# Layer 1 of a hybrid diffusion backbone: head outputs kept in SBUF, queries and key copies issued at other places, convolution outputs split later

## The chip, the cores and the metric

The kernel runs on one core of a Trainium2 chip. The time is that of the device, in microseconds (us), from the start of the program to its end. A core has five engines, each with its own in-order instruction stream: TensorE (PE, matrix products; its weight loads are listed apart as PEld), VectorE (DVE), ScalarE (ACT), GpSimd (POOL) and SyncE (SP, which here only issues transfers). An instruction whose operands are not ready holds up everything behind it on its engine. Transfers (DMAs) are issued from SP's and ACT's streams and run beside the engines. SBUF is the on-chip memory, PSUM the eight banks into which PE writes, DRAM the memory outside.

## The reference

Two layers over 1024 latent tokens of width 1024 and a prefix of 256 context tokens. Layer 0 holds two kinds of grouped-query attention and a projection. Layer 1, in which the edits lie, has a convolution branch C and a neighbourhood attention D over a grid of 16 rows and 64 columns:

```python
cv, cgl, cg, dq, dk, dv, dg = split_cols(h_lat @ w_in, ODD_WIDTHS)
oc = conformer_conv(cv, cgl, cg, dw_w, dw_b, ln_g, ln_b)
...
def d_row(args):      # one grid row of 64 queries; 8 heads
    kk = jnp.concatenate([c_dk, kr], axis=1)      # 256 context keys, 8 grid rows of keys
    vv = jnp.concatenate([c_dv, vr], axis=1)
    return gqa_attend(qr[:, :, :, None, :], kk, vv, bias).reshape(bsz, GRID_W, D_W)
...
y_lat = jnp.concatenate([oc, od * jax.nn.silu(dg)], axis=-1) @ w_out
x_lat = x_lat + g_l[:, None, :] * y_lat
```

`conformer_conv` is a depthwise convolution of 31 taps over 512 channels, a layer norm over the channels, and two SiLU gates. `gqa_attend` is softmax(q k / 8 + bias) v. All inputs and the output are float32; the output is an RMS norm of `x_lat`.

## The kernel before, in words

**Products in three parts.** Every float32 product is made of three matmuls on rounded numbers: `split` (line 294) writes the high part of a tile (a cast on ACT) and the low part (a subtraction on POOL, "g", or DVE, "v"), and `mm3` (line 315) issues high x high, high x low and low x high. So each tile that is to be multiplied costs an ACT cast and a POOL or DVE subtraction first, and both wait for the tile.

**Layer 1 in its order.** First the four blocks of the convolution's projection with the convolution itself (`conv_proj`, `conv_steps`, pool "cv"); then `d_proj(0)` and `d_proj(1)`, each of which projects q, k, v and gate of two of the eight heads and stores them in DRAM (QD, KD, VD, GD). Beside `d_proj(1)` runs the layer norm of the convolution (`ln_steps`, pool "ln"), whose result goes to DRAM too (Oc). Then the attention begins: 16 groups, each one head and one half of the grid's columns (`SEQ`). Three more pieces of work are woven between its steps by `weave`: `d_proj(2)`, `d_proj(3)`, and the output projection `out1_part`, first of the convolution's four blocks, then of the finished heads. `WV` holds how many steps of the attention go with each piece.

**One attention group.** `attn_prep` loads the group's queries (QH, QL), finds the row maxima on PE and DVE (`maxes`: product `mx`, then DVE's reductions with the bias tile `bm`), transposes them (`trn`) and writes them into QL, so that the softmax's shift is part of the score product. `attn_gen` then goes through seven tiles: two score matmuls `st` (QH with key tile KA, QL with key tile KB), the bias added on DVE (`pf`), the exponential on ACT, `split` into `ph` and `pl`, and some steps later three value matmuls `ov`. After the last tile `finish` divides, gates (`gt`) and stores. The preparation of group g+2 runs in the steps of group g. KB's upper part is a copy of KA on ACT (`load_k`, line 376), issued right behind the loads of KA, when the first group of the head before starts.

**Bounces through DRAM.** Each of the first six heads' outputs `y` is stored to O1d and comes back by `od_load`, which casts it on ACT. The convolution's outputs come back from Oc in `out1_alloc` and are split there, before the output projection is woven.

**What sets the order.** The program is handed to a scheduler which puts each engine's instructions into an order by priorities and by its own estimate of when each is ready; `later` and `issue_after` change a piece's priority or pin it behind a named instruction. So an edit at one place can move instructions at another, in layer 0 too. Memory pools lie on a stack: a tile whose bytes belonged to a pool before waits for the last use of those bytes. Of transfers on one stream, eight are under way at most (the ninth waits for the first's landing).

## Time and profile before

| | |
|---|---|
| time, median of 3 runs | 1595.98 us (1594.56 to 1597.62) |
| the profiled execution's own time | 1590.1 us |
| its span, first to last instruction | 1588.3 us |
| mean granted TensorE clock | 0.959 |
| busy: PE, PEld, DVE, ACT, POOL | 1477.4, 1178.0, 1087.8, 745.3, 791.0 us |
| first score matmul of layer 1's attention | at 1236.99 us of the span |
| bytes moved | 211.38 MB, mean 133 GB/s |

Times inside the program are microseconds from the start of the span. A row of the view by stretches gives, for each engine, the microseconds in which it was busy and the count of its instructions, then the granted clock (1.00 is full speed), and the share of time and rate of the transfers. A row of the view of waits names who waited, on what the wait ended, the sum, the number of times and the longest. A row of the chain has start, length and what ran; the chain follows back from the end to whatever released each step.

### The profile page before, as it was taken

The numbers are of one execution on the slowest core, as the hardware profiler recorded it, in microseconds if no ns is written. First come the engines' busy times: TensorE is split into PE (matmuls) and PEld (weight loads), VectorE is DVE, ScalarE is ACT, GpSimd is POOL, SyncE is SP. The second block draws the span as 40 slices with busy tenths as digits, with TensorE's granted clock in tenths as the row PEclk, the third lists the DMA queues.
The fourth block names the chain that finished last, engine by engine and source line by source line (L and its number), as shares of the span: only waits on it lengthen the run. The fifth ranks groups of instructions, "written<-read, shape, count | busy, mean of one in ns | idle before, by whom it ended". The sixth has DMA issues, their size and how long they took to land.

```text
span 1588.3 us, 21721 instructions
## 1 busy us (share of the span) xinstructions
PE 1477.4 (93%) x7084; PEld 1178.0 (74%) x7084; DVE 1087.8 (68%) x2283; ACT 745.3 (47%) x1418; POOL 791.0 (50%) x633
## 2 busy tenths in 40 slices
PE   6899999999999999999989879999998899899995
PEld 2785988886886778876866657888877778777775
DVE  2833576588599855566778857999566465778776
ACT  3722334443435555457555754433333454545563
POOL 3531352553445676557555755654431343344575
PEclk7899999998999999999999989999999899899997
DMA  9473324422312363212112032213546877988732
GB/s 366 157 238 121 110 84 152 137 76 90 110 50 82 99 210 101 64 57 65 30 38 80 7 101 60 80 54 101 190 160 198 234 222 215 273 243 239 224 101 106
DMA packets 159929, 211.38 MB, mean 133 GB/s; under 512 B 15356, under 2 KB 96456, under 8 KB 159816
## 3 DMA queue, kind: packets, MB, share of 16 engines
q1 hardware_dynamic: 153152, 198.42, 39.8%
q10 hardware_dynamic: 6664, 11.57, 2.2%
q8 instruction: 56, 0.92, 0.3%
q14 instruction: 57, 0.47, 0.1%
HBM read 153.84 MB, written 54.79 MB: 131 GB/s over the span
## 4 chain that ended last, share of the span: by engine, by line
PE 67%; DVE 16%; DMA 7%; issue 4%; ACT 2%; POOL 2%; SPq 0%; DVEq 0%; ACTq 0%; POOLq 0%
PE p L316 6%; PE p L317 6%; PE p L318 6%; PE ov L426 4%; PE ov L428 4%; PE ov L427 4%; PE st L463 4%; PE st L467 3%; PE po L316 3%; PE po L317 3%; PE po L318 3%; PE pq L316 3%; PE pq L317 3%; PE pq L318 3%; PE pg L318 2%
## 5 line engine op out<-in xcount | busy, mean ns | idle before, releaser
L299 POOL TENSOR_TENSOR pl<-pf,ph 128x512 fp32r<-128x512 f32 (+4 forms) x321 | 393.8, 1238 | 361.5 <-ACT ph L296 289.4
L299 POOL TENSOR_TENSOR wl<-wr,wh 128x512 fp32r<-128x512 f32 (+2 forms) x131 | 170.6, 1314 | 181.1 <-ACT wh L296 150.6
L475 ACT ACTIVATE pf<-st 128x512 f32<-128x512 f32 x284 | 165.6, 596 | 200.7 <-PE st L467 153.0
L296 ACT CAST ph<-pf 128x512 fp32r<-128x512 f32 (+4 forms) x364 | 209.6, 588 | 27.9 <-PE ov L427 17.7
L316 PE MATMUL p<-hh,wh 128*128 128x512 f32 x448 | 180.1, 402 | 8.6 <-ACT hh L296 2.8
L317 PE MATMUL p<-hl,wh 128*128 128x512 f32 x448 | 178.7, 400 | 0.9 <-POOL hl L299 0.9
L318 PE MATMUL p<-hh,wl 128*128 128x512 f32 x448 | 176.4, 400 | 0.0
L463 PE MATMUL st<-QH,KAt 128*128 128x512 f32 (+4 forms) x364 | 142.6, 393 | 10.0 <-ACT pf L475 8.1
L426 PE MATMUL ov<-ph,Vt 128*128 128x512 f32 (+4 forms) x364 | 141.3, 388 | 7.8 <-DVE y L625 6.2
L428 PE MATMUL ov<-pl,Vt 128*128 128x512 f32 (+4 forms) x364 | 141.6, 389 | 1.6 <-POOL pl L299 0.9
L427 PE MATMUL ov<-ph,Vt 128*64 128x512 f32 (+4 forms) x364 | 139.8, 384 | 0.0
L467 PE MATMUL st<-QL,KBt 68*128 68x512 f32 (+4 forms) x364 | 136.6, 388 | 0.0
L1041 DVE SCALAR_TENSOR_TENSOR cps<-U,taps,cps 128x512 f32<-128x512 f32 x184 | 126.4, 751 | 0.9
L296 ACT CAST wh<-wr 128x512 fp32r<-128x512 f32 (+2 forms) x134 | 81.1, 613 | 88.8 <-PE p L317 19.9
L316 PEld LDWEIGHTS p<-hh,wh 128*128 128x128 f32 x448 | 85.5, 191 | 31.3 <-ACT hh L296 3.0
L588 DVE TENSOR_REDUCE mp<-mx 128x1 f32<-128x512 f32 x128 | 85.9, 683 | 28.1 <-PE mx L587 27.5
L317 PEld LDWEIGHTS p<-hl,wh 128*128 128x128 f32 x448 | 85.1, 190 | 21.8 <-POOL hl L299 1.9
L318 PEld LDWEIGHTS p<-hh,wl 128*128 128x128 f32 x448 | 85.1, 190 | 19.9
L316 PE MATMUL pq<-wh,hh 128*128 128x384 f32 x256 | 88.4, 345 | 2.8 <-ACT hh L296 2.8
L463 PEld LDWEIGHTS st<-QH,KAt 128*128 128x128 f32 x364 | 70.1, 193 | 28.1 <-ACT pf L475 12.1
L426 PEld LDWEIGHTS ov<-ph,Vt 128*128 128x128 f32 x364 | 70.5, 194 | 23.9 <-issue 6.9
L428 PEld LDWEIGHTS ov<-pl,Vt 128*128 128x128 f32 x364 | 70.2, 193 | 24.1 <-POOL pl L299 5.0
(274 smaller groups left out, 3508.4 us busy)
## 6 DMA issues: line engine op xcount, KB each, us to landing
mw<-in_mod_w_dram SPq DMA_DIRECT2D x16, 1024.0 KB, 6.1
Q<-qs SPq DMA_DIRECT2D x40, 256.0 KB, 2.1
QH<-Q SPq DMA_DIRECT2D x80, 128.0 KB, 2.7
mw<-in_mod_w_dram SPq DMA_DIRECT2D x16, 512.0 KB, 7.1
wr<-in_od_d_dram SPq DMA_DIRECT2D x32, 256.0 KB, 2.9
wr<-in_ev_qkv_dram SPq DMA_DIRECT2D x16, 384.0 KB, 5.0
KAt<-KD SPq DMA_DIRECT2D x16, 384.0 KB, 5.5
wr<-in_od_wo_dram SPq DMA_DIRECT2D x22, 256.0 KB, 3.8
```

The costliest lines, as they stand in the source:

```text
L296: SC.copy(hi, src)
L299: (GP if leng == "g" else VE).tensor_tensor(lo, src, hi.bitcast(F32), op=ALU.subtract)
L316: PE.matmul(o, lh, rh, start=first, stop=False)
L317: PE.matmul(o, lh, rl, start=False, stop=False)
L318: PE.matmul(o, ll, rh, start=False, stop=last)
L426: PE.matmul(o, V[:, 64:192], ph[:, :n], start=(t == 0), stop=False)
L427: PE.matmul(g.ov[0:64, q0 : q0 + n], V[:, 0:64], ph[:, :n], start=False, stop=False)
L428: PE.matmul(o, V[:, 64:192], pl[:, :n], start=False, stop=(last and g.sink is None))
L463: sts.append(PE.matmul(st[:, :n], KA[:, cs], g.QH[:, q0 : q0 + n], start=True, stop=False))
L467: PE.matmul(st[:, :n], KB[0:68, cs], g.QL[0:68, q0 : q0 + n], start=False, stop=True)
L475: SC.activation(pf[:, :n], st[:, :n], AF.Exp, scale=1.0 if g.bias else SCALE)
L1041: VE.scalar_tensor_tensor(pc, uc, w, pc, op0=ALU.mult, op1=ALU.add)
```

## The change

It touches layer 1 in seven ways; layer 0's code computes as before.

- **Head outputs.** `yo`, a tile of 128 x 3 x 2 x 512 numbers, holds the outputs of heads 0 to 5 in SBUF. The twelve stores to O1d and the six loads from it go; `od_load` splits from `yo`.
- **Pools.** The pool `kvp`, which held small tiles and the queries for the whole program, now ends with layer 0. Layer 1 has its own pool "kv1". The exponentials' tiles (`pf`, `ph`, `pl`) and `yo` lie in a new pool "d0", which takes the bytes that the layer norm's pool used; the key, value and bias tiles stay in "d1", which now lies behind it.
- **Queries.** They are asked for when group g starts, for group g+3 (four buffers in place of three); the first three groups' before any preparation.
- **Maxima.** A preparation lets eight steps pass in place of four before its first maximum; `WV[0]` grows from 73 to 77.
- **Key copies.** The ACT copy KB<-KA no longer follows the loads; `copy_k` issues it in the middle of the head's predecessor's first group, pinned behind the last ACT instruction of the attention.
- **Convolution outputs.** `out1_alloc` only loads them; `out1_split` splits them after two steps of the weave, pinned in the same way, the low parts on POOL for the first half of the tokens and on DVE for the second (before: all on DVE).
- **Gate tiles of the layer norm** (`gc`) have two buffers in place of one.

```diff
-WV = (73, 53, 77, 24, 12)
+WV = (77, 53, 77, 24, 12)
...
+    acts = []
+
+    @contextmanager
+    def behind():
+
+        with tc.issue_after(acts[-1].ins):
+            yield
+
     def split(src, hi, lo, heng="s", leng="g"):
         if heng == "s":
-            SC.copy(hi, src)
+            acts.append(SC.copy(hi, src))
...
         SY.dma_start(KA[64:128, :].bitcast(F32), kl)
-        SC.copy(KB[0:64, :], KA[0:64, :].bitcast(F32))
+
+    def copy_k(k):
+        KA, KB = Ks[k % len(Ks)]
+        with behind():
+            acts.append(SC.copy(KB[0:64, :], KA[0:64, :].bitcast(F32)))
+
+    def queries(g, pool):
+
+        g.QH = pool.tile([P, 512], F32R, tag="QH", name=nm("QH"), bufs=4 if layer[0] else 3)
+        g.QL = pool.tile([P, 512], F32R, tag="QL", name=nm("QL"), bufs=4 if layer[0] else 3)
+        g.load_q(g.QH, g.QL)
 
     def attn_prep(pool, g):
...
-        for _ in range(4):
+        if layer[0]:
+            g.load_b()
+        else:
+            queries(g, pool)
+        QH, QL = g.QH, g.QL
+        for _ in range(8 if layer[0] else 4):
             yield
...
+        if layer[0]:
+            for g in groups[:3]:
+                queries(g, kvs[-1])
...
             if t == 0:
                 g.start()
+                if layer[0] and g.no + 3 < len(groups):
+                    queries(groups[g.no + 3], kvs[-1])
...
-                gc = vp.tile([P, 512], F32, tag="gc", name=nm("gc"), bufs=1)
+                gc = vp.tile([P, 512], F32, tag="gc", name=nm("gc"), bufs=2)
...
+        dlow = l1x.enter_context(tc.tile_pool(name="d0", bufs=1, reuse_waits="tile"))
+        yo = dlow.tile([P, 3, 2, 512], F32, tag="yo", name="yo")
         dpool = l1x.enter_context(tc.tile_pool(name="d1", bufs=1, reuse_waits="tile"))
...
             def gate():
                 g.gt = half("gt1")
                 SY.dma_start(g.gt[ds], GD[i][ds, hf])
+                if hf == 0 and hd < 7:
+                    copy_k(hd + 1)
...
-                y = half("y1")
+                y = half("y1") if i == 3 else yo[:, i, hf]
...
-                SY.dma_start(O1d[ds, i, hf], y[ds])
...
                     SC.dma_start(lo.bitcast(F32), Oc[:, f, c * 512 : (c + 1) * 512])
-                    split(lo.bitcast(F32), ocs[c][:, 0, f, :], lo, "s", OCE)
+
+        def out1_split():
+            for _ in range(2):
                 yield
+            for f in range(4):
+                for c in range(2):
+                    lo = ocs[c][:, 1, f, :]
+                    with behind():
+                        split(lo.bitcast(F32), ocs[c][:, 0, f, :], lo, "s", "gv"[c])
+                if f % 2:
+                    yield
...
             for f in range(3):
-                lo = od[hf][:, 1, f, :]
-                SY.dma_start(lo.bitcast(F32), O1d[:, f, hf, :])
-                split(lo.bitcast(F32), od[hf][:, 0, f, :], lo, "s", ODE)
+                split(yo[:, f, hf], od[hf][:, 0, f, :], od[hf][:, 1, f, :], "s", ODE)
...
-        run(out1_alloc())
-        weave(main, WV[2], out1_part(range(4)), 32, False, True, LAG[2])
+        out1_alloc()
+        weave(main, WV[2], chain(out1_split(), out1_part(range(4))), 36, False, True, LAG[2])
```

Three places show what the scheduler makes of it. The first is SP's stream beside `d_proj(1)`. `uc` and `gc` are loads of the layer norm, `GD` and `VD` stores of `d_proj(0)`, `wr` weights of `d_proj(1)`, and `KAt`, `bm`, `bs`, `Vt`, `gt` the first loads of the attention. Before:

```order
L1054 DMA uc_11336<-Uc 128x4x512
L1082 DMA gc_11505<-Gc 128x512
L1054 DMA uc_11604<-Uc 128x4x512
L1144 DMA GD_9742<-sgd_11211 256x1x256
L1163 DMA VD_9738<-spv_11251 128x768
L1163 DMA VD_9738<-spv_11251 128x256
L1163 DMA VD_9738<-spv_11259 128x512
L335 DMA wr_11317<-in_od_d_dram 128x512
L335 DMA wr_11323<-in_od_d_dram 128x512
L1243 DMA gt_2819_12122<-GD_9742 64x512
L1163 DMA VD_9738<-spv_11293 128x512
L335 DMA wr_11554<-in_od_d_dram 128x512
```

In the change, from the layer norm's second load on to the same weights (`wr_11557` here); of the rows between the two fences' pieces the loads of head 1's keys, values and gates are left out:

```order
L1081 DMA uc_11607<-Uc 128x4x512
L384 DMA KAt_11853<-KD_9735 64x1536
L385 DMA KAt_11853<-KD_9735 64x1536
L346 DMA wr_11320<-in_od_d_dram 128x512
L1259 DMA bm_11880<-in_d_bm_dram 128x440
L346 DMA wr_11326<-in_od_d_dram 128x512
L1259 DMA bm_11882<-in_d_bm_dram 128x320
L1269 DMA bs_12042<-in_d_bs_dram 128x256
L1269 DMA bs_12044<-in_d_bs_dram 128x352
L1269 DMA bs_12046<-in_d_bs_dram 128x512
```

The first two heads' keys, bias tiles, values and gates now stand ahead of the weights of the second half of `d_proj(1)`; before, the first `KAt` load stood 42 transfers behind those weights, after the layer norm's last store. On PE the first maximum (`mx`) of the attention stands 105 rows earlier, among the projections of `d_proj(2)`.

The second place is ACT's stream where the output projection is about to start. `oc` are the convolution's outputs, `pf` and `ph` the attention's exponentials and their high parts, `KBt` a key copy, `sgd` a gate of `d_proj(3)`. Before:

```order
L296 CAST oc_13961<-oc_13961 128x512
L1136 COPY vT_13483<-p_3237_13664 128x320 x2
L296 CAST oc_13961<-oc_13961 128x512
L473 ACTIVATE pf_13323<-pf_13323 128x320
L296 CAST oc_13961<-oc_13961 128x512
L473 ACTIVATE pf_13359<-pf_13359 128x224
L296 CAST ph_13321<-pf_13323 128x320
L296 CAST ph_13357<-pf_13359 128x224
L475 ACTIVATE pf_13388<-st_13383 128x512
L296 CAST ph_13386<-pf_13388 128x512
L376 CAST KBt_11847<-KAt_11846 64x1536
L1141 ACTIVATE sgd_13759<-p_3263_13760 128x512
```

In the change:

```order
L501 ACTIVATE pf_14021<-pf_14021 128x512
L307 CAST ph_14019<-pf_14021 128x512
L390 CAST KBt_11857<-KAt_11856 64x1536
L307 CAST oc_13957<-oc_13957 128x512
L307 CAST oc_13958<-oc_13958 128x512
L307 CAST oc_13957<-oc_13957 128x512
L307 CAST oc_13958<-oc_13958 128x512
L501 ACTIVATE pf_14056<-pf_14056 128x320
L501 ACTIVATE pf_14089<-pf_14089 128x224
```

The eight casts of `oc` stood among `d_proj(3)`'s copies and now stand behind it, some 15 tiles of the attention further on. PE has no other work that is ready without them: between the last matmul of `d_proj(3)` and the first of the output projection stood 51 matmuls of the attention, and now stand 100.

The third place is PE's stream near the end of layer 0, which no edit names. `st`, `ov` and `mx` are its attention's matmuls and `trs` the sums of a norm. Before:

```order
L587 MATMUL mx_8682<-KAt_543,QH_8628 128x512
L463 MATMUL st_8937<-QH_8320,KAt_543 128x512
L467 MATMUL st_8937<-QL_8321,KBt_538 128x512
L251 MATMUL trs_9247<-ones,acc_2243_8986 128x2 x4
L587 MATMUL mx_8696<-KAt_543,QH_8628 128x512
L426 MATMUL ov_8849<-ph_8717,Vt_544 128x512
```

In the change:

```order
L449 MATMUL ov_8849<-pl_8833,Vt_544 128x512
L491 MATMUL st_8937<-QH_8320,KAt_543 128x512
L495 MATMUL st_8937<-QL_8321,KBt_538 128x512
L614 MATMUL mx_8679<-KAt_543,QH_8628 128x512
L447 MATMUL ov_8849<-ph_8867,Vt_544 128x512
L448 MATMUL ov_8849<-ph_8867,Vt_544 64x512
L614 MATMUL mx_8682<-KAt_543,QH_8628 128x512
L254 MATMUL trs_9247<-ones,acc_2243_8986 128x2 x4
```

Twelve and more `ov` matmuls that stood behind the norm's sums now stand ahead of them. Shifts of this size, up to 37 places, run through the last eighth or so of layer 0; its last 50 or so matmuls of the output projection stand as before.

More of the change, by code (lines that the diff above doesn't have):

```diff
@@ L354, in silu2 @@
         VE.scalar_tensor_tensor(dst, dst, 1.0, psrc, op0=ALU.add, op1=ALU.mult)
[L357 to L358 removed]
+    bd = const("k_bd", [12, 4], SC)
     Ks, Vs = [], []
@@ L445, in attn_gen @@
                     yield
+        if layer[0]:
+            groups[0].copy()
         for gi, g in enumerate(groups):
@@ L972, in tile_kernel @@
     GD = [dram(f"GD{i}", [P, 2, 512]) for i in range(4)]
-    O1d = dram("O1d", [P, 3, 2, 512])
     with ExitStack() as l1x:
+        kvs.append(l1x.enter_context(tc.tile_pool(name="kv1", bufs=1, reuse_waits="tile")))
         wp = l1x.enter_context(tc.tile_pool(name="wp", bufs=1, reuse_waits="tile"))
```

28 lines of the change are left out of this document (12 added, 16 removed).

## The prediction

> **What bounds the kernel now.** I read the page first, then the view by stretches, then the chain of waits where a stretch loses time, then waits and groups there.
>
> ```profile
> span 1588.3 us, 21721 instructions
> PE 1477.4 (93%) x7084; PEld 1178.0 (74%) x7084; DVE 1087.8 (68%) x2283; ACT 745.3 (47%) x1418; POOL 791.0 (50%) x633
> ```
>
> PE is the bound, and the edits take no matmul from it. They can save only time in which PE stands or runs at a low clock. I call that a stretch's loss: its length less PE's busy time multiplied by the granted clock.
>
> ```profile
> core 0: us, PE busy (x) PEld busy (x) DVE busy (x) ACT busy (x) POOL busy (x), PEclk, DMA share, GB/s
> 800.00:870.00 70.00, 61.99 (x259) 46.10 (x257) 56.61 (x101) 39.99 (x72) 40.05 (x31) 0.94 0.21 66
> 870.00:935.00 65.00, 51.95 (x221) 36.09 (x221) 47.88 (x91) 44.52 (x88) 44.21 (x38) 0.89 0.04 13
> 1140.00:1160.00 20.00, 18.66 (x95) 15.04 (x94) 5.96 (x9) 6.20 (x13) 10.65 (x8) 1.00 0.72 232
> 1230.00:1256.00 26.00, 20.76 (x91) 16.68 (x90) 9.44 (x25) 8.96 (x15) 10.35 (x10) 0.80 0.92 251
> 1256.00:1368.00 112.00, 109.15 (x562) 90.16 (x561) 71.16 (x171) 58.82 (x120) 42.06 (x40) 1.00 0.77 228
> 1368.00:1380.00 12.00, 9.09 (x49) 8.21 (x48) 7.16 (x19) 6.75 (x13) 5.82 (x5) 0.73 0.94 247
> 1380.00:1396.00 16.00, 14.50 (x61) 11.35 (x61) 11.61 (x31) 7.47 (x16) 7.82 (x7) 0.78 0.91 274
> 1396.00:1494.00 98.00, 91.80 (x444) 73.36 (x442) 73.66 (x175) 49.59 (x96) 48.31 (x45) 1.00 0.82 235
> ```
>
> Losses: 26 − 20.76 × 0.80 = 9.4 us where the attention of layer 1 begins (1230 to 1256), 12 − 9.09 × 0.73 = 5.4 at 1368 to 1380, 98 − 91.80 = 6.2 in the output projection's first part (1396 to 1494), and 70 − 61.99 × 0.94 = 11.7 and 65 − 51.95 × 0.89 = 18.8, together 30.5, in layer 0's tail. The stretch 1256 to 1368 shows what undisturbed weaving loses: 2.85 us in 112, 2.5%.
>
> **The change part by part.** *First loads earlier (term A).* At the attention's start the chain goes through SP, not PE:
>
> ```profile
> 1228.94 0.49 SPq L374
> ...
> 1229.48 6.70 DMA KAt<-KD
> ...
> 1237.60 0.43 PE p L318
> ...
> 1241.24 5.29 DMA bm<-in_d_bm_dram
> ...
> 1247.67 0.39 PE trn L404
> ```
>
> ```profile
> PE trn L404 <- DVE nmt L394: 2.9, 1, 2.9
> PE mx L1259 <- DMA KAt<-KD: 1.8, 1, 1.8
> ```
>
> The first key load is issued at 1228.94, so late that the maxima, and through the bias load the transpose `trn`, find PE waiting: 2.9 + 1.8 = 4.7 us idle, and after it matmuls of 0.43 us. In the change these loads stand ahead of weights that before went out at 1157, some 70 us earlier, and the first `mx` stands 105 rows earlier in the middle of projections that can cover DVE's part. If all of it goes, the stretch loses 2.5% of 26, 0.7, and A is 9.4 − 0.7 = +8.7. Bounds: +4.7 (the idle time alone, the clock stays low) and +9.4. I take 8.7, because low clock stands only where PE has stood.
>
> The Trainium skill, "TensorE: Matmul & The Clock Gate", section "What's actually happening", has it that the clock is either half or full, decided anew in free-running windows of about 3.4 us. The trace agrees on the two speeds: `p` takes 0.43 us here and 0.24 at 1362.00 below. By its window one such stall would add a single window at half rate, an estimated 1.7 us, so that A would be 4.7 + 1.7 = 6.4 and the sum 2.3 lower, 6.0; the trace's 0.80 over 26 us is 4.2 us, so I keep the row.
>
> *Key copies pinned (term B).*
>
> ```profile
> 1362.00 0.24 PE p L316
> ...
> 1365.61 4.28 DMA KAt<-KD
> ...
> 1369.92 0.66 ACT KBt L376
> ...
> 1371.30 0.60 ACT sgd L1141
> ...
> 1371.92 0.76 DVE sgd L1143 x2
> ...
> 1372.81 0.42 PE trv L1151 x2
> ```
>
> ```profile
> ACT KBt L376 <- DMA KAt<-KD: 17.4, 7, 5.9
> ACT od L296 <- DMA od<-O1d: 9.8, 5, 3.2
> ...
> PE trv L1151 <- DVE sgd L1143: 2.0, 1, 2.0
> PE po L316 <- ACT od L296: 1.8, 1, 1.8
> PE st L463 <- DVE pf L472: 1.7, 4, 0.8
> ...
> PE mx L1259 <- DMA QH<-QD: 0.8, 2, 0.5
> PE p L316 <- DVE r L438: 0.8, 1, 0.8
> ```
>
> The copy KB<-KA waits on ACT for its load (17.4 us in seven waits; PE mostly has other work meanwhile). At 1365 it has the last gate `sgd` of `d_proj(3)` behind it; DVE and then PE's `trv` wait for that gate, 2.0 us. Pinned in the middle of the preceding group, the copy is issued when its load has long landed, and what follows it on ACT is exponentials that it holds up for one copy, 1.5 us by the group below, under cover of the weave's other matmuls (without that cover the 1.5 us would be PE's, once a head). B is the wait, 2.0, and half of the clock's 9.09 × 0.27 = 2.5, since the next stretch has a low clock of its own: +3.2. Bounds +2.0 and +5.4.
>
> *Outputs in SBUF, queries a group ahead (term D).* PE's wait on `od` (1.8; ACT's five for the same loads sum to 9.8) ends with the bounce, that on QH (0.8) with the earlier request, and that on `r` (0.8, behind another key copy): +3.4. Bounds: 0, when DVE, busy 73.66 of 98 us, holds PE at the same places, and 6.2 + 0.8 = 7.0. O1d's twelve stores and six loads and `gc`'s second buffer touch no wait on the path; they count as nothing, and would cost nothing without cover.
>
> *Convolution outputs split later (term C, a cost).*
>
> ```profile
> L376 ACT CAST KBt<-KAt 64x1536 fp32r<-64x1536 f32 x6 | 8.9, 1479 | 11.5 <-DMA KAt<-KD 11.5
> ...
> L299 DVE TENSOR_TENSOR oc<-oc 128x512 fp32r<-128x512 f32 x8 | 5.3, 680 | 2.5 <-ACT oc L296 2.4
> ...
> L296 ACT CAST oc<-oc 128x512 fp32r<-128x512 f32 x8 | 4.9, 617 | 5.0 <-DMA oc<-Oc 5.0
> ```
>
> Between `d_proj(3)` and the output projection PE has only the attention, whose tiles go round PE, DVE, ACT and back. That stretch (1380 to 1396) takes 16 / 61 = 0.262 us a matmul, the woven one behind it 98 / 444 = 0.221. It grows from 51 to 100 matmuls: 49 × 0.041 = 2.0 us. Into it now fall the eight casts, 8 × 0.617 = 4.9 us on ACT, and half of the low parts on DVE, 4 × 0.68 = 2.7; before, they were covered. ACT is busy 7.47 of 16 us there and DVE 11.61, so most finds room: I put 2 of these 7.6 on the path. C is −4.0, bounds −2.0 and −2.0 − 7.6 = −9.6. The four low parts on POOL, half idle there, are off the path.
>
> *What the early loads delay (term F, a cost).* The weights of the second half of `d_proj(1)` now stand behind 3.9 MB more: four key loads of 384 KB, two value loads of 320, five bias tiles of 832 together, two `bm` of 380, two gates of 128 and a `gc` of 256 (the tiles of the SP rows shown above, at 4 bytes an element).
>
> ```profile
> 1157.03 2.04 SPq L335 DMA_DIRECT2D wr<-in_od_d_dram  x2
> ...
> 1170.36 0.62 ACT L296 CAST wh<-wr 128x512 fp32r<-128x512 f32 x1
> ```
>
> ```profile
> wr<-in_od_d_dram SPq DMA_DIRECT2D x32, 256.0 KB, 2.9
> VD<-spv SPq DMA_DIRECT2D x16, 256.0 KB, 3.1
> ```
>
> Issued until 1159.07, landing 2.9 later, they are there at 1162.0, and first cast at 1170.36: 8.4 us of slack. Alone, 3.9 MB at 251 GB/s take 15.5 us: 7.1 too many. But the queues had room: 20 us at 232 GB/s are 4.6 MB from 1140 to 1160, so 8.5 MB go before the weights land; at 274 GB/s, the fastest of these rows, that is 31 us (1171), at 251 34 us (1174): 0.6 to 3.6 late. F is −3.0, bounds 0 and −7.1.
>
> *The rest.* No edit touches layer 0's arithmetic, but its tail is reordered by up to 37 places; I take 0 (the rival below has its price). Four more steps of delay before a maximum and four more in `WV[0]` cancel on paper.
>
> Sum: 8.7 + 3.2 + 3.4 − 4.0 − 3.0 = 8.3 us. With all terms at their good ends it would be 9.4 + 5.4 + 7.0 − 2.0 = 19.8, with all at their bad ones 4.7 + 2.0 + 0 − 9.6 − 7.1 = −10.0. The profiled execution took 1590.1 us, 5.9 below the median of the runs; I take the saving from both: 1581.8 for a profile, and 1596.0 − 8.3 = 1587.7, so 1588 us.
>
> **The rivals.** *More comes back.* The three losses go wholly (9.4 + 5.4 + 7.0), C stays 4.0 and the weights land in time: 17.8 us, 1578. For it: each loss has a named transfer at its root. Against: DVE's 73.66 of 98 us.
>
> *The waits change their name.* A pays its idle time alone (4.7), and where ACT was late DVE is next: `st` already waits for `pf`, and `trn` for `nmt`, both DVE's. B and D give nothing: 4.7 − 4.0 − 3.0 = −2.3, 1598. Against it: at 1256 to 1368 DVE is busy for 71.16 of 112 us and PE loses 2.5%.
>
> *The weights are late in full.* SP issues in order, and a value load must wait for its store, which in this region can be long:
>
> ```profile
> 1143.78 9.81 DMA VD<-spv
> ```
>
> If SP stands at `Vt` until then, F is −7.1: 4.2 us gained, 1592. Against it: the median of such stores is 3.1 us, by the row above.
>
> *The clock falls in the longer stretch.* It has 0.78 now. At half speed throughout, its 49 more matmuls take 0.43 in place of 0.221 us, 10.2 where C had 2.0, 8.2 more: 0.1 us gained, 1596. Against it: the granted clock there may still be that of the stall at 1368 before it. The Trainium skill, same page, section "A second HAM failure mode: psum-queue depth-cycling", says that short idle gaps between groups of matmuls, without any long stop, can make the clock swing; no row here parts the two causes.
>
> *Slower: layer 0's tail.* It loses 30.5 us of 135 in a loop of PE, ACT and DVE with hardly any transfers (0.04 to 0.21 of the share), so the order alone decides. If the new one loses half as much again, 15 us, the time is 1588 + 15 = 1603. It decides from a loss of 30.5 + 8.3 + 3 = 42 us in 800 to 935 upward. For it: twelve and more `ov` now stand ahead of the norm's sums, which the stretch's end waits for. Against it: no more work is in it, and the order could as well be better.
>
> **How the numbers follow.** Forecast 1588, its own range 1580 to 1594: 0.45. More comes back: 0.12. Waits change their name: 0.13. Weights late: 0.10. Clock: 0.07. Layer 0: 0.13. Two differences below 0.2% (3.2 us; faster is then below 1592.8, slower above 1599.2) can't be told apart here. Faster: 0.37 of the forecast, 0.12, 0.02, 0.04 and 0.01, 0.56. Slower: 0.01, 0.02, 0.01, 0.01 and 0.11, 0.16. The same: the remaining 0.28. The range reaches up to most of layer 0's case and down to the first rival: 1577 to 1602.
>
> **What would show it.** A: no wait of PE on KAt or of `trn` on `nmt` where the attention starts, and a granted clock near 1.00 there. B: no wait of ACT on KAt anywhere, none of `trv` on `sgd`. D: no rows of O1d, and less than 3 us lost in the first 98 of the output projection. C: the stretch without projections lasts some 26 us in place of 16; its clock tells the clock rival. F: waits of ACT's `wh` on `wr` at about 1170, of not over 3 us. Layer 0: 800 to 935 as long as before within 3 us. The prediction is wrong if that last stretch moves by more, if SP stands at a value load, or if the stretch without cover takes more than 30 us.

## The result, and the profile after

The changed kernel takes 1580.66 us (median of 4 runs, 1578.79 to 1581.59) where the kernel before, on the same chip, takes 1595.27 (4 runs, 1590.73 to 1597.62): 14.6 us less, a ratio of 0.9906 with a 95% interval of 0.9885 to 0.9926. It is faster, and by more than the 8.3 us forecast. The profiled execution took 1581.6 us, only 8.5 less than the profiled execution of before (1590.1).

Page and view by stretches of the changed kernel:

```profile
span 1579.8 us, 21684 instructions
PE 1469.3 (93%) x7084; PEld 1172.7 (74%) x7084; DVE 1086.9 (69%) x2279; ACT 748.8 (47%) x1418; POOL 794.1 (50%) x637
```

```profile
800.00:870.00 70.00, 63.49 (x265) 46.78 (x264) 56.19 (x104) 42.73 (x76) 39.96 (x31) 0.95 0.20 66
870.00:935.00 65.00, 50.47 (x217) 35.90 (x214) 48.62 (x89) 43.11 (x85) 43.79 (x38) 0.89 0.04 13
...
1140.00:1160.00 20.00, 16.37 (x84) 12.81 (x82) 2.11 (x5) 3.24 (x7) 7.62 (x6) 0.99 0.92 276
1160.00:1200.00 40.00, 39.02 (x178) 31.85 (x179) 26.93 (x43) 17.14 (x31) 12.29 (x9) 0.92 0.84 235
...
1230.00:1256.00 26.00, 26.00 (x136) 22.07 (x135) 11.44 (x31) 11.57 (x24) 9.28 (x8) 1.00 0.55 166
...
1368.00:1380.00 12.00, 10.88 (x66) 8.19 (x64) 10.01 (x24) 8.60 (x18) 6.58 (x6) 1.00 0.94 300
1380.00:1396.00 16.00, 11.44 (x44) 8.53 (x44) 9.90 (x25) 7.91 (x16) 8.73 (x8) 0.68 0.78 220
1396.00:1494.00 98.00, 94.81 (x448) 77.11 (x449) 77.27 (x177) 52.23 (x100) 56.22 (x50) 0.97 0.72 205
```

The attention's start (1230 to 1256) loses nothing now; before it lost 9.4 us. The stretch 1368 to 1380 has its clock back. New losses stand at 1140 to 1200, where PE has 16.37 of 20 us and then a clock of 0.92, and at 1380 to 1396: 16 − 11.44 × 0.68 = 8.2 us, before 4.7.

How far the same matmul has moved against the kernel before is read from the timelines (the same: the one with the same number in the order of the `p`, or of the `po`). The first column is its start in the kernel before, the others how much later (+) or earlier (−) it starts in the changed kernel and in seven of the experiments below (in their order: late loads, the kernel before with gc's second buffer, late loads with one such buffer, late loads with three bm buffers, the changed kernel with key copies and with convolution outputs issued early, the fastest variant; `p` are the projections of layer 1, `po` the output projection; the first `po` alone is no fixed place, since attention passes it):

```
place               before  after  late loads  before+gc2  late,gc1  late,bm3  copy early  oc early  fastest
first p              948.9   +0.1     -1.5        +3.8       -1.0      -0.8       -2.3       -1.8      -2.2
p in d_proj(1)      1150.6   +0.1     -1.6        +3.8       -1.1      -0.9       -2.3       -1.7      -2.2
p, 14 us on         1164.0   +6.0     -3.2        +2.2       -2.1      -2.5       +3.7       +4.3      -3.8
p before attention  1211.4   +2.9     -6.4        -1.0       -2.2      -5.7       +0.6       +1.2      -7.0
p behind its start  1265.5   -4.9    -13.0        -8.8       -1.1     -10.8       -5.5       -6.7     -11.2
p in d_proj(3)      1348.5   -5.9    -11.2       -11.9       -5.2     -13.6       -6.4       -8.2     -14.0
last p              1380.6   -8.5    -15.4       -11.9      -10.2     -17.6       -8.3      -11.1     -17.5
first po            1394.7  +11.7    +12.5        -5.8      +16.8      +0.1      +12.3      -12.5     -23.4
po, half way        1489.7   -5.6     -5.1        -2.8       -0.5     -12.9       -2.2      -14.8     -23.1
last po             1572.0   -8.3     -7.6        -3.2       -2.6     -15.0       -4.1      -14.6     -23.4
```

In the changed kernel 5.9 us are lost in d_proj(1) between 1150 and 1164, 3.1 come back until 1211, 7.9 are won at the attention's start, 1.0 until 1348, 2.5 at the end of d_proj(3), and 0.2 are lost from there to the end. The start of this table is also a warning: layer 0 is the same code in all columns, and its end lies anywhere from −2.3 to +3.8. One profiled execution is good to some 3 us as a whole, and better only from one place to the next.

What is lost in d_proj(1) is a wait for weights. The chain there, ACT's timeline, and PE's longest waits from 1140 to 1262 (the second of them lies behind 1200):

```profile
1148.68 11.55 DMA wr<-in_od_d_dram
```

```profile
1160.31 0.62 ACT L307 CAST wh<-wr 128x512 fp32r<-128x512 f32 x1 [8.22 <-DMA wr<-in_od_d_dram]
```

```profile
PE p L327 <- ACT wh L307: 4.5, 1, 4.5
PE p L327 <- DVE spq L1128: 2.6, 1, 2.6
```

These are the third and fourth weights of the first block (q and k); the third stands right behind the first key loads on SP. Issued at 1148.68, 2.9 us being the median of their kind before, the first took 11.55, beside the layer norm's second load of 1 MB and 768 KB of keys.

### The profile page after: what moved, and what is told of

Same layout as the page of the kernel before. It is cut to its first block, busy times and chain, and to the rows that moved or that the text cites. A ratio compares the mean times of both kernels' runs of the same rounds, so it can differ in the third digit from the quotient of the medians.

```text
span 1579.8 us, 21684 instructions
## 1 busy us (share of the span) xinstructions
PE 1469.3 (93%) x7084; PEld 1172.7 (74%) x7084; DVE 1086.9 (69%) x2279; ACT 748.8 (47%) x1418; POOL 794.1 (50%) x637
## 4 chain that ended last, share of the span: by engine, by line
PE 73%; DVE 15%; DMA 6%; ACT 2%; issue 2%; POOL 1%; SPq 0%; ACTq 0%; DVEq 0%; POOLq 0%
PE p L327 6%; PE p L328 6%; PE p L329 6%; PE ov L447 4%; PE ov L449 4%; PE po L327 4%; PE po L329 4%; PE po L328 4%; PE ov L448 4%; PE st L491 4%; PE st L495 4%; PE pq L327 3%; PE pq L328 3%; PE pq L329 3%; PE pg L329 2%
## 5 line engine op out<-in xcount | busy, mean ns | idle before, releaser
L329 PE MATMUL pq<-wh,hl 128*128 128x384 f32 x256 | 87.4, 341 | 0.0
```

The lines of the kernel that those rows point to most:

```text
L329: PE.matmul(o, ll, rh, start=False, stop=last)
```

## The experiments

All were timed in five rounds; the ratio is to the kernel before on the same chip, whose median in the five calls was 1592.6 to 1595.9. Times of different calls can differ by that much without a cause in the kernel; where the intervals of two ratios overlap, the text says so. In the diffs, + is the experiment.

**The same two kernels again.** No edit.

> The kernel before, timed against itself, with a second profile. The timed runs of before lay at 1590.7 to 1597.6 us, its profiled execution at 1590.1; the change saved 14.6 us by the medians (1595.3 to 1580.7) but only 8.5 by the two profiles (1590.1 to 1581.6). Theory T (the edits explain 8.5, and before's own executions differ by some 6 us): ratio 1.000 within 0.002, and this profile, if it is one of the longer ones, shows its extra 4 to 7 us in one or two stretches in which PE waits for transfers (1200 to 1256 most likely). Rival R (the edits explain all 14.6, and the first profile of before was a lucky one in the stretches that were changed): extra time in 1230 to 1396 alone. A third way: a lower granted clock in layer 0.

> The changed kernel again. All theories: ratio 0.988 to 0.993, about 1580.7 us. If the 14.6 us came from the few runs of before, the ratio is nearer to 0.9947 (8.5 us).

The kernel before against itself: 1.0002 (0.9989 to 1.0015), 1594.5 us, runs from 1591.6 to 1600.1. The changed kernel: 0.9913 (0.9898 to 0.9927), 1580.7 us, runs from 1578.3 to 1582.9, profile 1580.7. So the 14 us are real. The second profile of before took 1593.0:

```profile
span 1591.2 us, 21721 instructions
```

2.3 of its 2.9 us more are there when layer 0 ends, and 1.7 arise between 1211 and 1265; behind that the difference lies between 2.5 and 4.1. Neither R's place nor T's holds it. Over all calls the kernel before ran from 1588.0 to 1600.8 us; both its profiles (1590.1, 1593.0) lie in the lower half of that, and of its 80 timed executions three took no longer than the first profile; both profiles of the changed kernel (1581.6, 1580.7) lie within a microsecond of its median. The difference of two profiles is therefore short of the difference of the medians. Why the kernel before scatters more, and where its longer executions lose, is open: none of them was traced.

**Late loads.** The bias, key and value tiles in front, on the bytes of the layer norm, as before:

```diff
-        dlow = l1x.enter_context(tc.tile_pool(name="d0", ...))
-        yo = dlow.tile([P, 3, 2, 512], F32, tag="yo", name="yo")
         dpool = l1x.enter_context(tc.tile_pool(name="d1", ...))
+        dlow = l1x.enter_context(tc.tile_pool(name="d0", ...))
+        yo = dlow.tile([P, 3, 2, 512], F32, tag="yo", name="yo")
```

> The changed kernel with its two pools in the other order (key, value and bias tiles in front, on the layer norm's bytes): the first loads of the attention are late again, all other edits stay. Theory T: the 6.0 us that d_proj(1) lost come back and the 12.5 us gained at the attention's start go: 6.5 us slower than the changed kernel, about 1587. Rival R (the gain is that of the pinned copies and of the outputs in SBUF, and the two effects of the early loads cancel): within 2 us of the changed kernel, 1579 to 1583.

0.9915 (0.9900 to 0.9929), 1580.5 us: the same as the changed kernel. Theory T fell. By the table the loss in d_proj(1) is gone (−1.6 to −3.2 in place of +0.1 to +6.0), and the attention's start is won nevertheless, 6.6 us from 1211 to 1265, though the first key load goes out at 1217.85 in place of 1146.32 (the 12.5 us of the expectation are 10.9 in the table, from 1164 to 1265). What is ahead by 7 us at the last `p` is then given back in front of the output projection.

**Weights first.** In the changed kernel the attention's loads are pinned behind the fourth weight transfer of d_proj(1):

```diff
+        pin = wrs[-5].ins      # wrs: the weight transfers so far
...
+        with tc.issue_after(pin):
             load_head(0)
+        with tc.issue_after(pin):
             weave(main, WV[0], d_proj(2), 31, False, True, LAG[0])
```

> The changed kernel with the attention's first loads pinned behind the fourth weight transfer of d_proj(1) on SP's stream. Theory T (the 6.0 us lost in d_proj(1) are a wait of ACT's wh for these weights, 8.2 us in the profile, since key and bias loads are ahead of them): the wait goes, 4 to 6 us come back, 1575 to 1577. Rival (the transfers of that stretch are too many in any order: DMA share 0.92): the wait goes over to the layer norm's load or to the next weights, 1580 to 1582.

0.9921 (0.9905 to 0.9936), 1582.3 us: no gain, the rival. PE's wait changes its name and ends some 17 us later: it is now for the split of k, whose cast on ACT waits 7.6 us for a store of q (PE's waits from 1140 to 1262; the second row lies behind 1200, where the changed kernel has 2.6):

```profile
PE p L328 <- DVE spk L311: 7.3, 1, 7.3
PE p L328 <- DVE spq L1129: 3.9, 1, 3.9
PE p L328 <- ACT wh L308: 0.9, 1, 0.9
```

**The layer norm's gate buffer.** The late loads had come 11 us earlier than before the change, behind the same store of the layer norm. So one number was tried alone in the kernel before, and the reverse in the variant with late loads and in the changed kernel:

```diff
-                gc = vp.tile([P, 512], F32, tag="gc", name=nm("gc"), bufs=1)
+                gc = vp.tile([P, 512], F32, tag="gc", name=nm("gc"), bufs=2)
```

> The kernel before with one number changed: two buffers in place of one for the layer norm's gate tiles gc. Theory G (before, the attention's first key load stands on SP behind the layer norm's last store, and the layer norm ran at 4.4 us a step because each gate load waited for the multiplication before it; with two buffers it ends some 9 to 11 us earlier, so that the loads are early enough): the stall at 1230 to 1256 goes, 8 to 12 us faster, ratio 0.992 to 0.995. Rival Q (the gain at the attention's start comes from the queries asked for earlier and the later maxima): within 2 us of before.

> The changed kernel with the pools in the other order (late first loads, as in the run before of that name), and the layer norm's gate tiles back to one buffer. Theory G: the first key load is at 1226 or later again and the stall returns: 5 to 10 us slower than with two buffers, 1586 to 1590. Rival Q: within 2 us of it, 1579 to 1582, since the later maxima wait in any case.

> The changed kernel itself (early first loads), with gc back to one buffer. The prediction counted gc's second buffer as nothing. Theory G1 (gc matters only where the first loads stand behind the layer norm, as before and with the late loads): with early loads it is worth little, within 2 us of 1580.7. Rival G2 (the layer norm's end itself holds something else, its DVE steps or the queue): 3 to 7 us slower.

In the kernel before it gives 0.9930 (0.9915 to 0.9944), 1583.3 us: 12.1 us by one number. Taken from the late variant it costs 6.6 (1587.1, 0.9953, 0.9939 to 0.9968). SP's timeline shows the mechanism, of the kernel before and then with two buffers:

```profile
1214.66 0.33 SPq L1089 DMA_DIRECT2D Oc<-uc  x1
1215.04 0.42 SPq L1082 DMA_DIRECT2D gc<-Gc  x1
1219.00 0.32 SPq L1089 DMA_DIRECT2D Oc<-uc  x1
...
1223.60 0.33 SPq L1089 DMA_DIRECT2D Oc<-uc  x1
...
1228.03 0.32 SPq L1089 DMA_DIRECT2D Oc<-uc  x1
1228.94 0.49 SPq L374 DMA_DIRECT2D KAt<-KD  x1
```

```profile
1215.23 0.33 SPq L1089 DMA_DIRECT2D Oc<-uc  x1
...
1216.13 0.40 SPq L1089 DMA_DIRECT2D Oc<-uc  x1
...
1220.54 0.32 SPq L1089 DMA_DIRECT2D Oc<-uc  x1
...
1222.22 0.46 SPq L1089 DMA_DIRECT2D Oc<-uc  x1
1223.28 0.50 SPq L374 DMA_DIRECT2D KAt<-KD  x1
```

With one buffer each gate load waits for the multiplication that stands before its store, 4.4 us a step; with two, a pair of steps takes about 5. In a run whose first `Oc` of the half is 0.6 us later the key load is 5.7 us earlier, and that is enough: in the table 7.8 us are won between 1211 and 1265, against 1.1 lost with late loads and one buffer, where the key load is at 1228.86 again. Another 4.8 us are won ahead of it, from 1150 to 1211, where PE's wait for a norm's factors (`bc` on DVE's `nr`) falls from 2.6 to 1.0 us. In the changed kernel, where nothing waits for the layer norm's last store, taking the buffer away makes it faster: 1575.9 us, 0.9884 (0.9865 to 0.9903), 4.8 us less, which none of the theories expected (the two intervals overlap, the times of the runs do not). The same weights go out at 1149.79 there, no earlier than in the changed kernel. d_proj(1) loses 2.3 us in place of 5.9 until 1164, but 5.5 in place of 2.9 until 1211, and 12.3 in place of 7.9 are won from there to 1265. What of this is the 256 KB fewer ahead and what the scheduler's other order, no run tells.

**Four steps before the first maximum.**

```diff
-        for _ in range(8 if layer[0] else 4):
+        for _ in range(4):
...
-WV = (77, 53, 77, 24, 12)
+WV = (73, 53, 77, 24, 12)
```

> The changed kernel with the pools in the other order, four steps in place of eight before a preparation's first maximum and WV[0] = 73 in place of 77, as before. Theory G: within 2 us of 1580.5. Rival Q (the later maxima give the loads time): 5 to 10 us slower, PE waits on KAt or trn at the attention's start.

In the late variant: 0.9932 (0.9915 to 0.9950), 1584.0 us, 3.5 more, between the two forecasts, and the intervals overlap. At the attention's start PE waits 0.2 us; so the later maxima are not what keeps it clear.

**A third buffer for the bias tiles.** The new loss at 1380 to 1396 is read in the changed kernel by DVE's and PE's waits from 1366 to 1412, and by finer stretches:

```profile
DVE mx L1301 <- DMA bm<-in_d_bm_dram: 4.7, 2, 2.7
...
PE st L491 <- DVE pf L500: 4.3, 4, 2.7
PE trn L425 <- DVE nmt L415: 3.5, 1, 3.5
```

```profile
1377.90:1381.30 3.40, 2.17 (x8) 0.99 (x7) 2.20 (x5) 0.00 (x0) 0.80 (x1) 1.00 0.94 325
1381.30:1384.40 3.10, 0.00 (x1) 0.00 (x1) 2.07 (x8) 2.53 (x6) 2.03 (x3) 0.50 0.95 323
1384.40:1391.55 7.15, 6.87 (x19) 5.09 (x20) 5.85 (x13) 3.04 (x7) 4.18 (x4) 0.50 0.73 199
1391.55:1396.00 4.45, 3.70 (x22) 2.97 (x20) 1.77 (x5) 2.34 (x4) 2.52 (x2) 1.00 0.69 160
```

A preparation needs three bias tiles and has two buffers; the third load starts when the first has been used, at 1377.31, and lands 4.8 us later. In the kernel before DVE has no wait for `bm` there. In the longer stretch without projections PE stands for 3.5 us (1380.87 to 1384.40, the `trn` row), and the clock is at half from 1381.3 to 1391.55. That wait had begun only 0.4 us earlier; whether it or the shorter gaps ahead of it, with PE busy for 2.17 of 3.40 us, brought the clock down, the rows do not say.

```diff
-                bms[b] = dpool.tile([P, 440], F32, tag="bm", name=nm("bm"), bufs=BMB)[:, :n]
+                bms[b] = dpool.tile([P, 440 if b == 1 else 320], F32, tag="bm" if b == 1 else "bn", name=nm("bm"),
+                                    bufs=1 if b == 1 else 2)[:, :n]
```

> The changed kernel with the pools in the other order, and a third buffer for the bias tiles bm of the maxima (one of 440 columns, two of 320). Between the last projection and the first output projection DVE waits for bm, 2.6 us, whose load starts only when the buffer's last use has ended, and PE then runs at half clock. Theory: with a third buffer these waits go, 3 to 5 us faster, 1576 to 1577. Rival (DVE and ACT bound the attention in that stretch anyway, or the transfers are too many): within 1.5 us, 1579 to 1582.

> The kernel before with two buffers for gc and three for the bias tiles bm, nothing else. With gc alone it took 1583.3 us, the full change 1580.7, the full change with late loads and three bm buffers 1577.4. Theory G (nearly all of the change's worth is the gc buffer, and bm adds 3): 1580 to 1581. Rival (pinned copies, split and outputs in SBUF carry a part that bm's third buffer does not replace): 1583 or more, as with gc alone.

On the late variant: 0.9892 (0.9875 to 0.9910), 1577.4 us, 3.1 less (the two intervals overlap, the times of the runs do not), and DVE's wait for `bm` (2.6 us there) is gone from that stretch. On the kernel before with two gate buffers: 0.9921 (0.9894 to 0.9947), 1581.8 us, 1.5 less, inside the interval. Two buffer counts in the old kernel come within 1.1 us of the whole change by the times (by the ratios 0.9921 and 0.9906); against the rival (1583 or more) the interval is too wide to say more.

**Convolution outputs split early again.**

```diff
                     SC.dma_start(lo.bitcast(F32), Oc[:, f, c * 512 : (c + 1) * 512])
+                    split(lo.bitcast(F32), ocs[c][:, 0, f, :], lo, "s", "v")
+                yield
...
-        weave(main, WV[2], chain(out1_split(), out1_part(range(4))), 36, False, True, LAG[2])
+        weave(main, WV[2], out1_part(range(4)), 32, False, True, LAG[2])
```

> The changed kernel with late first loads and three bm buffers (1577.4 us), the convolution's outputs split in out1_alloc again, low parts all on DVE, as before. Theory of the prediction's term C (the later split costs 4 us, since it lies in the stretch without cover): 2 to 4 us faster, 1573 to 1575. Rival (the stretch lasts as long as the attention's own steps and transfers, whatever is in it): within 1.5 us.

> The changed kernel itself, with the convolution's outputs split in out1_alloc, as before the change. The prediction put the later split at a cost of 4.0 us (2.0 to 9.6); with late loads and three bm buffers it cost 6.3 us. Theory: 4 to 7 us faster than the changed kernel, 1574 to 1577. Rival (the cost depends on the third bm buffer, without which the stretch is bound by bm's loads): within 2 us.

With late loads and three bm buffers: 0.9861 (0.9836 to 0.9887), 1571.1 us, 6.3 less, the intervals just overlapping. In the changed kernel: 0.9894 (0.9875 to 0.9912), 1578.4 us, 2.3 less, inside the interval. With the heads' outputs through DRAM as well (below) the early split makes 1564.7 us of 1572.6, 7.9 less, and there the intervals are apart. So the later split costs, as the prediction said; in the changed kernel alone that is not clear of the noise. Between the last projection and the first output product lie 34.3 us in the changed kernel, 12.8 with the early split; its stretch has a full clock:

```profile
1370.00:1384.00 14.00, 10.66 (x51) 7.33 (x49) 10.19 (x26) 8.35 (x17) 8.95 (x8) 1.00 0.99 288
1384.00:1396.00 12.00, 11.49 (x59) 9.51 (x60) 9.12 (x22) 6.80 (x13) 7.41 (x6) 1.00 0.82 233
```

**Key copies right behind their loads again.**

```diff
         SY.dma_start(KA[64:128, :].bitcast(F32), kl)
+        SC.copy(KB[0:64, :], KA[0:64, :].bitcast(F32))
...
-                if hf == 0 and hd < 7:
-                    copy_k(hd + 1)
```

> As the run before of this set, with the convolution's outputs split late, and the key copies KB<-KA issued right behind their loads again. Term B of the prediction (the pinned copy saves 2 to 5 us, ACT's wait for the key loads): 1580 to 1582. Rival (PE has other work during these waits): within 1.5 us of 1577.4.

> The changed kernel itself, with the key copies KB<-KA issued right behind their loads, as before the change. The prediction put their pinning at 3.2 us (2.0 to 5.4). With late loads and three bm buffers it was worth 9.5 us. Theory: 6 to 10 us slower than 1580.7, since the copy holds up ACT at each head's start, not at one place. Rival: 2 to 5 us, as predicted, the rest is due to the other pools' order.

With late loads and three bm buffers: 0.9952 (0.9934 to 0.9970), 1586.9 us, 9.5 more. In the changed kernel: 0.9944 (0.9927 to 0.9962), 1585.7 us, 5.0 more, as its rival said. ACT's waits of the latter from 1215 on, and PE's waits in it at the end of d_proj(3) (1358 to 1382) and then behind 1375:

```profile
ACT KBt L386 <- DMA KAt<-KD: 16.8, 6, 4.2
```

```profile
PE trv L1177 <- DVE sgd L1169: 0.4, 1, 0.4
```

```profile
PE ov L448 <- DMA Vt<-VD: 3.6, 1, 3.6
...
PE st L490 <- ACT pf L502: 2.5, 1, 2.5
```

So the pinning is worth what B said or more, but not where B had it: with the copies early again, PE's wait of `trv` on the gate is 0.4 us, not 2.0, and the last `p` stands where it stands in the changed kernel (−8.3 against −8.5). The 4 us are lost behind it, where ACT waits for its key loads as before, and PE for exponentials and a value load. On the variant the loss is ahead of the last `p`: 9.3 us there (−8.3 against −17.6).

**Head outputs through DRAM again.**

```diff
-                y = half("y1") if i == 3 else yo[:, i, hf]
+                y = half("y1")
...
+                SY.dma_start(O1d[ds, i, hf], y[ds])
...
-                split(yo[:, f, hf], od[hf][:, 0, f, :], od[hf][:, 1, f, :], "s", ODE)
+                lo = od[hf][:, 1, f, :]
+                SY.dma_start(lo.bitcast(F32), O1d[:, f, hf, :])
+                split(lo.bitcast(F32), od[hf][:, 0, f, :], lo, "s", ODE)
```

> The changed kernel with late first loads and three bm buffers, the six heads' outputs stored to DRAM and loaded again before their split, as before. Part of term D of the prediction (a wait of 1.8 us of the output projection for od): 2 us slower, 1579. Rival (hidden): within 1.5 us of 1577.4.

> Late first loads, three bm buffers, convolution outputs split early, and the heads' outputs stored and loaded again. Alone, the early split gave 6.3 us and the bounce 4.8 over 1577.4. If they add: 1566 to 1568. If both gains come from the same stretch without cover: within 2 us of 1571.

> The changed kernel itself, with the six heads' outputs stored to DRAM and loaded again, as before the change. The prediction put the wait that this edit ends at 1.8 us. On two variants with late loads the bounce was faster, by 4.8 and 6.4 us. Theory (outputs in SBUF cost, since their pool takes bytes or moves instructions): 2 to 6 us faster than 1580.7. Rival (a matter of those variants' order): within 2 us, or up to 2 slower.

With late loads and three bm buffers: 0.9873 (0.9848 to 0.9897), 1572.6 us, 4.8 less where the theory had 2 more, but the intervals overlap. With the early split too: 0.9811 (0.9788 to 0.9833), 1564.7 us, 6.4 less than with outputs in SBUF, and the fastest of all: the two gains add. In the changed kernel: 0.9924 (0.9904 to 0.9944), 1582.5 us, within the interval of the changed kernel's; but without `yo` its pool is smaller and the key tiles lie elsewhere: the first key load goes out at 1218.67, as with late loads, so that this run must be held against the late variant (1580.5): no difference. Outputs in SBUF gain nothing in any of the three.

**The queries.** The fastest variant with queries asked for in the preparation, three buffers, four steps and WV[0] = 73:

```diff
-        if layer[0]:
-            for g in groups[:3]:
-                queries(g, kvs[-1])
...
-                if layer[0] and g.no + 3 < len(groups):
-                    queries(groups[g.no + 3], kvs[-1])
...
+        queries(g, pool)
```

> The fastest variant (late first loads, three bm buffers, convolution outputs split early, heads' outputs by DRAM: 1564.7 us), with the queries asked for in the preparation again, three buffers, four steps before the first maximum, WV[0] = 73, as before. So of the change only gc's second buffer, the pinned key copies and the exponentials' own pool are left, with bm's third buffer. Theory (copies, gc and bm carry the gain, the earlier queries the 0.8 us that PE waited for QH and the four steps some 3): 1566 to 1569. Rival (the early queries are what frees the queue at each group's start): 1572 or more.

0.9851 (0.9829 to 0.9872), 1571.5 us: 6.8 more, between the two forecasts, the intervals just overlapping. But little of it is the price of the queries. By the trace 7.0 us of the 7.8 that the two profiles differ by are there at 1150, ahead of any attention of layer 1: its first `p` starts at 959.8 in place of 946.7, although the last matmul of layer 0 starts at 947.8, only 1.4 us later. In the fastest variant the first projections cover the norm between the layers; here the norm's matmuls stand ahead of them, PE waits, and the clock falls. The fastest variant, then this run:

```profile
947.00:960.00 13.00, 13.00 (x68) 10.87 (x67) 2.57 (x7) 0.77 (x2) 1.02 (x1) 1.00 0.21 68
```

```profile
947.00:960.00 13.00, 6.69 (x31) 6.03 (x30) 5.33 (x8) 2.50 (x4) 4.75 (x4) 0.62 0.40 141
```

No edit names that place, and what turned the order there is not known. Behind it the run loses 1.8 us more between 1211 and 1265, and at the last `po` the whole difference is 7.8.

The fastest variant is the changed kernel with the pools in the other order, the bias tiles in three buffers, and two of the seven edits undone (outputs in SBUF, later split). It beats both kernels: 1564.7 us, 1.9% under the kernel before. Page and stretches, where the changed kernel had 8.2 us of loss:

```profile
span 1562.7 us, 21723 instructions
```

```profile
1372.00:1380.00 8.00, 8.00 (x41) 6.51 (x40) 6.09 (x13) 4.62 (x10) 6.06 (x6) 1.00 1.06 335
1380.00:1396.00 16.00, 15.86 (x78) 12.78 (x77) 13.04 (x31) 9.62 (x18) 8.47 (x9) 1.00 1.04 275
```

## Why the prediction was right and wrong

**The sum held for the profile, in part by luck, and failed for the median.** Its terms came to 8.3 us, and the two profiled executions differ by 8.5. Place by place they agree too: 7.9 us at the attention's start (A: 8.7), −2.9 ahead of it (F: −3.0), 3.5 from there to the last `p` (B: 3.2), −0.2 behind that (C and D: −0.6). But undone one by one the edits were worth other amounts, as shown below, and the errors made up for each other.

The step that failed is the carrying: "The profiled execution took 1590.1 us, 5.9 below the median of the runs; I take the saving from both". The runs show that a profiled execution of the kernel before lay 1.5 and 5.9 us under its medians, in both traces, while those of the changed kernel lay on theirs; the medians differ by 14.6 and 13.9 us. The text had the 5.9 before it and took it for a constant that both kernels share. The variant with late loads and one gate buffer shows the same gap, without the early loads: its profile (1586.8) is 3.3 us under the first of before, where B, C and D came to 2.6, and its median 8.3 (5.1 to 9.7 by the ratio). So the terms were worked out on an execution of before that was among its shortest. Where its usual ones lose the 5 us more is not known. Within the sum, the step that failed is the gate buffer, put at nothing (A, next).

**A (8.7 forecast): size right, cause half right.** Between 1211 and 1265 the changed kernel wins 7.9 us. The stall was that of late key loads, and it goes when they are earlier. But the pool edit, which the term was booked on, is not needed: with late loads and gc's second buffer 6.6 us are won at the same place, with that buffer alone in the old kernel 7.8, and 12.1 in its whole time. (With early loads the buffer is not needed: without it the changed kernel takes 1575.9.) The sentence that "`gc`'s second buffer touch no wait on the path" is the wrong one. The row that speaks against it was the kernel's own: the key load's place right behind the layer norm's last store on SP, at 1228.94, and that store's spacing of 4.4 us. I looked at where the loads stood, not at what held the queue in front of them. The view of DVE's waits of the kernel before, from 1150 to 1240, had it, in its second row:

```profile
DVE uc L1088 <- DMA gc<-Gc: 9.2, 5, 3.7
```

**F (−3.0): measured −5.9 by 1164, and the wrong weights.** Of the 5.9 us 3.1 come back before 1211, but that is the gate buffer's doing: 3.2 are won there with it in the old kernel and with late loads, 0.1 with late loads and one buffer. The term was worked out for the second block's weights at 1170; those were in time. Late were the first block's third and fourth, at 1160, which the order already showed right behind the key loads; they had no slack, since before the change ACT had waited 0.9 us for them. The share of transfers (0.92 at 276 GB/s in 1140 to 1160) is the bound by bytes that the term spoke of, and with the weights first another transfer, a store of q, held PE up instead.

**A and F together: nothing.** Early loads and late loads give 1580.7 and 1580.5 us. That 7 us won before the last projection do not reach the end is shown by the table; that the third bias buffer brings 3.1 of them back is likely, by times that do not overlap and intervals that do; what takes the rest is not known.

**B (3.2): 5.0 on the changed kernel, 9.5 on a variant, at other places.** The wait of `trv` that carried the term (2.0 us) is 0.4 without the pinning, and gone with it. ACT's waits for key loads are gone with it and back without it, so the mechanism (a copy that waits on ACT holds what is behind it) stands; at which instruction it costs PE its 5 us, the waits show only in part.

**C (−4.0): right in sign, within its bounds.** Undoing it gave 2.3 us in the changed kernel, inside the noise, 6.3 on the variant, and 7.9 on that variant with the bounce. The stretch without projections grew to 34.3 us, more than the 26 forecast and the 30 named as the point from which the prediction would be wrong: beside what the term counted, the third bias tile, hidden before, stood in it with 4.7 us of DVE's wait, and the clock was at half beside it. That is not the whole of the cost, since with the third buffer the later split still cost 6.3 us. How the rest divides between the casts and the stretch's length no run tells.

**D (3.4): not confirmed.** Outputs in SBUF gain nothing in three comparisons, and cost 4.8 us (inside the noise) and 6.4 us (clear of it) in two. The wait of 1.8 us for `od` was in the trace of before; that its end let another wait come is likely, and not shown. The queries' 0.8 us are not tested cleanly: the run without them took 6.8 us more, but all except some 1 us of that arose at the start of layer 1. The four steps, which the text let cancel on paper, were worth 3.5 us in the late variant, with overlapping intervals.

**The rivals.** The clock rival had the right place: half clock from 1381.3 to 1391.55, 10.25 us of a stretch of 34.3, where it priced half clock throughout. What set it off stays open, as the prediction left it. The Trainium skill, "TensorE: Matmul & The Clock Gate", section "What's actually happening", puts a return to full speed at about 3.4 us of sustained work; here PE was busy for 6.87 of the 7.15 us from 1384.40 on, with gaps of some 0.2 us, and full speed came only at the end of them. The rival of layer 0 fell: 800 to 935 loses 70 − 63.49 × 0.95 + 65 − 50.47 × 0.89 = 29.8 us, before 30.5. The weights came late at another place than their rival said, and SP did not stand at a value load.

## What to carry to other kernels

Before a load is moved, look at what the queue in front of it waits for: here a second buffer for a small gate tile, one number, gave 12.1 of the 14.6 us by itself in the old kernel. Edits that share a queue or a stretch do not add: the same buffer was worth 12.1, 6.6 and −4.8 us in three surroundings, and two of the change's seven edits cost time or gave none, so that each edit has to be timed in the kernel that is to be kept. Such a run has to be read by place as well: of the 6.8 us that the run without early queries lost, nearly all lay where none of its edits is. And a saving worked out on one profiled execution belongs to that execution: with a scatter of 13 us in the one kernel and of 5, over fewer runs, in the other, the difference of medians was nearly twice that of the profiles.

## What was not expected of the hardware

A transfer of 256 KB that had a median of 2.9 us took 11.55 us behind 1.8 MB on the same queues. Where PE stood for 3.5 us the granted clock was 0.50 for 10.25 us (1381.3 to 1391.55), longer than the wait itself, and in the last 7.15 us of that PE was busy for 6.87. And the last matmul of layer 0, the same code throughout, started between 944 and 952 us in traces of kernels that differ in layer 1.
